# A hybrid decoder step on one core: fewer, longer steps in the mixers' first stage, and small products in four quarters of the array

## The chip, the cores and the metric

The kernel runs on one core of one Trainium2 chip. The metric is the device time of one execution in microseconds (us); the median of the runs is compared. A core has TensorE (PE: matrix products into PSUM, which has eight banks here), VectorE (DVE), ScalarE (ACT), GpSimd (POOL) and SyncE (SP), whose queue issues nearly all DMAs of this kernel. Each engine runs its own instructions in the order in which they were built, and waits on semaphores for the others. TensorE's clock is granted at one of two levels, 1.2 or 2.4 GHz; the profile prints the grant as a share of 2.4 GHz.

## The reference

One layer of a decoder over 2048 prompt tokens and 8 sample tokens, width 1024:

```python
h = rmsnorm(x, norm_mix)
p = h @ w_in                                  # 31 tiles of 128 columns are kept
y_a = gdn_mixer(p_a)     # gated delta rule: conv, decay, chunks of 64, triangular solve
y_b = rwkv_mixer(p_b)    # RWKV-7: token shift, data-dependent decay, state update per token
y_c = hgrn_mixer(p_c)    # forget gate, chunks of 64, gated norm
x = x + concat(y_a, y_b, y_c) @ w_out
h = rmsnorm(x, norm_ffn)
x = x + (silu(h @ w_gate) * (h @ w_up)) @ w_down     # hidden width 2816
y = rmsnorm(x, norm_final)
```

The three mixers carry a 64x64 state per head from chunk to chunk, and the states are outputs too. All is fp32 in and out.

## The kernel before

**Products.** Every large product is done as three fp32r matmuls (hi x hi, hi x lo, lo x hi; lines 377 to 379, in `mm3`), 128x128 weights against up to 512 columns. The tokens are cut into four quarters `q` of 512 (the last has 520, done as two pieces of 260). A quarter has 31 tiles of the input projection (`proj`, tile `psp`), the output projection (`out_proj`, 8 tiles `pso`, which read the mixers' results back from DRAM, `s_mix`, as `mxs`), and the feed-forward part (`ffn`: 22 tiles `pfg` and `pfu`, and `pd`). In matmuls that is 31 x 24 + 8 x 24 + 22 x 48 + 3 x 8 x 22 = 2520 a quarter; counted over the program 7560 of 512 columns and 5040 of 260. All four quarters' projections come first, then for each quarter the output projection and the feed-forward part.

**Mixers.** Each quarter has eight units: three of `gdn` (names with `_g`), three of `rwkv` (`_r`), two of `hgrn` (`_h`); the digits in a built name are the quarter and the unit, so `px_g22` belongs to quarter 2, unit 2. A unit is a Python generator with a first stage (all that needs no state: `first()`), for `gdn` and `rwkv` a stage that inverts 64x64 triangles through DRAM (`inverse`), a second stage that walks the eight chunks in a chain (`px`, `pv`, `pS`, each a small matmul and then a VectorE step), and an output part. Each `yield` ends a step. The eight sample tokens have units of their own (`gs`, `rs`, `hs`), started beside quarter 2's.

**Order.** `Driver.turn` lets each live unit take one step, at most one unit (for the third kind of stage two) in a stage, and then asks the products' generator for as many matmuls as `RATES[q]` says:

```python
        self.due += self.rate
        while self.made < self.due and self.product():
            pass
```

`RATES` (line 1428) is 12.25, 14.25, 15.25 and 19.25 for the four quarters. A quarter's output projection is asked for only when its units are done (`D.left[q]`). This written order is a priority and not yet the order of the engines: the recording layer lays the instructions out on a planned timeline (`schedule_with_timeline_sim=True`), where TensorE takes a later product whenever the earlier small matmuls are not ready. The order that comes out of this is fixed in the program.

**Small matmuls.** They are fp32, and the hardware runs each as two passes, so the trace has two records for one. Their operands have 64 or 32 partitions and sit in a part of the array: partitions 0 to 63 of a 64x64 operand with PSUM partitions 0 to 63 take one quarter of the array, 64 to 127 with 64 to 127 the quarter diagonal to it. `pair` (line 255 on) does head 0 and head 1 of a pair in those two quarters. `hgrn` has five levels (spans 32, 16, 8, 4, 2), each a scaled copy `lv`, eight pairs into one bank `pl`, and one predicated copy on VectorE (line 1217). `rwkv` makes `pa` in the two diagonal quarters and, later, `pk` in the two others. First-stage tiles in PSUM share two banks (tag `A`).

Of the kernel before, what the change touches and what calls it, by code (L numbers as in the profile page):

```python
# [14 lines left out]
ALU = mybir.AluOpType  # L15
# [10 lines left out]
C = 64  # L26
G = 512
GC = G // C
# [63 lines left out]
class Kern:  # L92
# [645 lines left out]
    def half(self, pair, h, other=False):  # L738

        return self.heads(pair[h], other)(h)  # L740
# [39 lines left out]
    def gdn(self, q, u):  # L780

        nc = self.nc
# [5 lines left out]
        def first():  # L788
# [17 lines left out]
            sums, made = {}, None  # L806
# [26 lines left out]
            yield  # L833
# [3 lines left out]
            nc.vector.scalar_tensor_tensor(t, beB, -1.0, L, ALU.mult, ALU.mult)  # L837
            N = ch(self.T(f"N_{nm}"))

            Q = [ch(self.T(f"Q{h}_{nm}")) for h in range(2)]  # L840
            for c0 in range(0, GC, 4):
# [7 lines left out]
                yield  # L849
            inv = self.inverse(N, ("g", u, q), nm)  # L850
            next(inv)
            yield
# [7 lines left out]
            yield  # L860
# [3 lines left out]
            nc.vector.tensor_tensor(ch(dl), k3, ch(dl), ALU.mult)  # L864
            kd = ch(self.T(f"kd_{nm}"))
# [110 lines left out]
    def rwkv(self, q, u, lo):  # L976
# [7 lines left out]
        def first():  # L984
# [6 lines left out]
            nc.tensor.matmul(ps, lhsT=self.w2a2[0:64, us], rhs=wa[0:64], start=True, stop=True)  # L991
            self.rwkv_decay(lw, ps, u)
            nc.vector.tensor_tensor_scan(cu, self.reset, lw, 0.0, ALU.mult, ALU.add)
            yield
# [13 lines left out]
            yield  # L1008
# [3 lines left out]
            a = self.T(f"a_{nm}")  # L1012
            ps = self.ps(f"paa_{nm}")
            nc.tensor.matmul(ps, lhsT=self.w2a2[64:128, us], rhs=wa[64:128], start=True, stop=True)
            self.rwkv_rate(a, ps, u)
            yield
# [21 lines left out]
            def att(l3, swap, outs, name):  # L1038

                for c0 in range(0, GC, 4):  # L1040
                    ps = self.ps(f"p{name}_{nm}").rearrange("p (c w i) -> p c w i", w=2, i=C)
                    for c in range(4):
# [4 lines left out]
                    for w in range(2):  # L1047
                        for to, p in outs(w):
                            to, at, n = to[:, c0:c0 + 4], ps[p, :, w], p.stop - p.start
                            m = lambda x: x[p, None, :].to_broadcast([n, 4, C])  # L1050
                            if w == 0:
                                nc.vector.tensor_tensor(to, at, m(self.nstrict), ALU.mult)
                            else:
                                nc.vector.scalar_tensor_tensor(to, m(self.neg), 0.0, at, ALU.is_ge, ALU.mult)
                    yield

            NR = [ch(self.T(f"{n}_{nm}")) for n in ("N", "Rb")]
            yield from att(a3, 0, lambda w: ((NR[w], slice(0, 128)),), "a")
            N, Rb = NR
            inv = self.inverse(N, ("r", u, q), nm)  # L1060
            next(inv)
            yield

            W = [[ch(self.T(f"W{w}{h}_{nm}")) for h in range(2)] for w in range(2)]
            yield from att(k3, 1, lambda w: [(half(W[w], h, True), slice(64 - 64 * h, 128 - 64 * h))
                                             for h in range(2)], "k")
# [7 lines left out]
            self.tr_tok(self.heads(kt, True), k, f"ptk_{nm}")  # L1074
            yield
# [7 lines left out]
            nc.vector.tensor_tensor(a3, a3, fb, ALU.mult)  # L1083
            yield
# [78 lines left out]
    def hgrn(self, qi, u):  # L1163
# [7 lines left out]
        def first():  # L1171
# [27 lines left out]
            yield  # L1199
            for n, s in enumerate((32, 16, 8, 4, 2)):  # L1200
# [12 lines left out]
                yield  # L1213
                ps = ch(self.ps(f"pl_{nm}"))
# [8 lines left out]
            for h in range(2):  # L1223
                nc.vector.tensor_tensor(half(W, h), ch(q)[H[h]], ch(eb)[H[h]], ALU.mult)
                nc.vector.tensor_copy(half(W, h, True), att[H[h]])
# [202 lines left out]
RATES = (12.25, 14.25, 15.25, 19.25)  # L1428
# [224 lines left out]
```

## Time and profile before

| what | before |
|---|---|
| median of 3 runs | 3200.33 us (3198.95 to 3200.74) |
| profiled execution | 3198.47 us, its span 3196.7 us |
| TensorE busy | 3085.4 us, 97% of the span |
| VectorE busy | 2192.8 us, 69% |
| ScalarE busy | 1189.0 us, 37% |
| mean granted clock | 0.983 |

The span runs from the first to the last instruction; the profiled execution's own time lies 1.8 us over it. Busy time of TensorE is the union of its matmuls, whose ends are modelled: a matmul of 512 columns is shown as some 0.39 us long while the next starts after 0.23. So costs on TensorE are read from one start to the next, not from the durations.

### The profile page before, as it was taken

How to read it: one execution, taken by the hardware profiler on the slowest of the kernel's cores; microseconds unless marked ns; L12 is line 12 of the kernel's file. 1: busy time of each engine (PE TensorE's matmuls, PEld its weight loads, DVE VectorE, ACT ScalarE, POOL GpSimd, SP SyncE). 2: the span in 40 equal slices, each digit the busy share in tenths (PEclk: the TensorE clock that was granted, in tenths of full speed). 3: DMA queues.
4: the chain of work that ended last, by engine and by line, in shares of the span. 5: the costliest groups of instructions: out<-in, count | busy, mean ns of one | idle time of the engine just before them, and what ended most of it. 6: DMA issues, size and time to landing. Idle time of an engine off the chain costs nothing.

```text
span 3196.7 us, 62530 instructions
## 1 busy us (share of the span) xinstructions
PE 3085.4 (97%) x24812; PEld 2469.9 (77%) x24812; DVE 2192.8 (69%) x5369; ACT 1189.0 (37%) x2056; POOL 10.2 (0%) x21
## 2 busy tenths in 40 slices
PE   5989999999999999999999999999999999999998
PEld 3767767777888767677777777777777778999998
DVE  4885666678667788986898887778766654443334
ACT  3543143235325444644365435254532312221002
POOL 0000000000000000000000000000000000000000
PEclk8989999999999999999999999999999999999999
DMA  9958657656655766677775445565645456755552
GB/s 233 333 187 272 186 177 215 187 167 183 198 162 184 229 212 204 221 226 251 227 226 185 162 158 170 168 184 183 205 162 165 149 207 210 249 173 185 185 185 90
DMA packets 393074, 628.06 MB, mean 196 GB/s; under 512 B 176653, under 2 KB 181005, under 8 KB 392781
## 3 DMA queue, kind: packets, MB, share of 16 engines
q1 hardware_dynamic: 391692, 622.99, 61.0%
q8 instruction: 195, 3.19, 0.4%
q10 hardware_dynamic: 1088, 1.07, 0.1%
q14 instruction: 99, 0.80, 0.1%
HBM read 456.79 MB, written 167.19 MB: 195 GB/s over the span
## 4 chain that ended last, share of the span: by engine, by line
PE 79%; DVE 9%; DMA 6%; ACT 3%; SPq 1%; issue 1%; DVEq 0%; ACTq 0%
PE psp L377 7%; PE psp L378 7%; PE psp L379 7%; PE pd L377 5%; PE pd L378 5%; PE pd L379 5%; PE pfu L378 5%; PE pfg L377 4%; PE pfu L377 4%; PE pfu L379 4%; PE pfg L378 4%; PE pfg L379 4%; PE pso L378 1%; PE pso L377 1%; PE pso L379 1%
## 5 line engine op out<-in xcount | busy, mean ns | idle before, releaser
L377 PE MATMUL psp<-xs,w_in 128*128 128x512 f32 (+1 forms) x1240 | 446.3, 360 | 29.2 <-ACT xs L409 17.5
L378 PE MATMUL psp<-xs,w_in 128*128 128x512 f32 (+1 forms) x1240 | 445.9, 360 | 0.3 <-DVE xs L410 0.3
L379 PE MATMUL psp<-xs,w_in 128*128 128x512 f32 (+1 forms) x1240 | 442.9, 357 | 0.8 <-DVE w_in L333 0.8
L377 PEld LDWEIGHTS psp<-xs,w_in 128*128 128x128 f32 x1240 | 235.5, 190 | 72.6 <-ACT xs L409 19.7
L379 PEld LDWEIGHTS psp<-xs,w_in 128*128 128x128 f32 x1240 | 235.6, 190 | 39.5 <-issue 4.4
L378 PEld LDWEIGHTS psp<-xs,w_in 128*128 128x128 f32 x1240 | 235.4, 190 | 39.1 <-issue 2.9
L591 DVE TENSOR_TENSOR x<-pd,x 128x512 f32<-128x512 f32 (+1 forms) x240 | 138.3, 583 | 115.6 <-PE pd L379 113.9
L377 PE MATMUL pfg<-xhs,w_wg 128*128 128x512 f32 x496 | 201.8, 407 | 3.9 <-ACT w_wg L332 2.3
L379 PE MATMUL pfu<-xhs,w_wu 128*128 128x512 f32 x496 | 198.7, 401 | 1.4 <-DVE w_wu L333 1.2
L378 PE MATMUL pfg<-xhs,w_wg 128*128 128x512 f32 x496 | 198.6, 400 | 0.7 <-DVE xhs L549 0.7
L378 PE MATMUL pfu<-xhs,w_wu 128*128 128x512 f32 x496 | 199.2, 402 | 0.0
L377 PE MATMUL pfu<-xhs,w_wu 128*128 128x512 f32 x496 | 198.6, 400 | 0.3 <-ACT w_wu L332 0.3
L379 PE MATMUL pfg<-xhs,w_wg 128*128 128x512 f32 x496 | 198.0, 399 | 0.8 <-DVE w_wg L333 0.8
L377 PE MATMUL pd<-u,w_wd 128*128 128x512 f32 x464 | 188.3, 414 | 6.4 <-ACT u L362 2.3
L378 PE MATMUL pd<-u,w_wd 128*128 128x512 f32 x464 | 187.2, 404 | 0.4 <-DVE u L363 0.2
L379 PE MATMUL pd<-u,w_wd 128*128 128x512 f32 x464 | 185.1, 400 | 0.0
L570 ACT ACTIVATE t<-t 128x512 f32<-128x512 f32 (+1 forms) x110 | 60.0, 546 | 305.3 <-DVE t L569 301.7
L286 ACT ACT_TABLE_LOAD x91 | 116.8, 1283 | 113.6 <-PE oss_g L276 22.1
L362 ACT ACTIVATE u<-t 128x512 fp32r<-128x512 f32 (+1 forms) x110 | 59.9, 545 | 221.1 <-DVE t L573 220.2
L473 DVE TENSOR_TENSOR p<-psp,ri 128x512 f32<-128x512 f32 (+1 forms) x155 | 90.3, 583 | 73.2 <-PE psp L379 71.3
L572 DVE SCALAR_TENSOR_TENSOR t<-pfu,rf 128x512 f32<-128x512 f32 (+1 forms) x110 | 64.2, 583 | 102.9 <-PE pfu L379 100.0
L569 DVE TENSOR_TENSOR t<-pfg,rf 128x512 f32<-128x512 f32 (+1 forms) x110 | 64.2, 584 | 91.3 <-PE pfg L379 83.2
(638 smaller groups left out, 7368.9 us busy)
## 6 DMA issues: line engine op xcount, KB each, us to landing
w_in<-sw_in SPq DMA_DIRECT2D x186, 512.0 KB, 3.9
w_wg<-sw_wg SPq DMA_DIRECT2D x80, 512.0 KB, 3.5
w_wu<-sw_wu SPq DMA_DIRECT2D x80, 512.0 KB, 3.3
w_wd<-sw_wd SPq DMA_DIRECT2D x72, 512.0 KB, 3.3
sw_in<-w_in SPq DMA_DIRECT2D x62, 512.0 KB, 5.1
s_p<-p SPq DMA_DIRECT2D x93, 256.0 KB, 4.3
sw_wg<-w_wg SPq DMA_DIRECT2D x44, 512.0 KB, 2.9
sw_wu<-w_wu SPq DMA_DIRECT2D x44, 512.0 KB, 3.7
```

The lines of the kernel that those rows point to most:

```text
L286: p = self.nc.scalar.preload_act_table_set("natural_log_exp_and_others")
L362: nc.scalar.activation(out[:, 0], src, AF.Copy)
L377: nc.tensor.matmul(ps, lhsT=hi[:, ws], rhs=xs[:, 0, xc], start=start, stop=False)
L378: nc.tensor.matmul(ps, lhsT=hi[:, ws], rhs=xs[:, 1, xc], start=False, stop=False)
L379: nc.tensor.matmul(ps, lhsT=lo[:, ws], rhs=xs[:, 0, xc], start=False, stop=stop)
L473: nc.vector.tensor_tensor(p[:, c0:c0 + cn], ps, rstd[q][:, c0:c0 + cn], ALU.mult)
L569: nc.vector.tensor_tensor(g, psg, r[:, cs], ALU.mult)
L570: nc.scalar.activation(t, g, AF.Tanh, scale=0.5)
L572: nc.vector.scalar_tensor_tensor(p, psu, 0.5, r[:, cs], ALU.mult, ALU.mult)
L591: nc.vector.tensor_tensor(x2[d][:, c0:c0 + cn], ps, x2[d][:, c0:c0 + cn], ALU.add)
```

## The change

It rewrites the first stage of all mixers in 78 steps a quarter instead of 118 (yields are taken out, and what stood between them runs on), and raises `RATES` so that more matmuls are asked for after a turn. In `gdn` the sum of squares of one part is started behind the convolution of the next. In `rwkv` the rate `a` is made beside the decay, and `pa` and `pk` are made in one loop, in turns, into two banks, which fills all four quarters of the array. In `hgrn` a level's scaled copy is made one step ahead, and its pairs go to two banks: even chunks in the diagonal quarters, odd chunks in the other two; so there are two predicated copies of half the size, and the final copies `W` are split in two. No matmul is added or taken away.

```diff
@@ gdn first
+            def total():
+                which, sq = pend
+                sums[which] = self.bsum(f"ss_{nm}", sq), sq
+                return made or self.mm
...
-                yield
+                if pend:
+                    made = total()
                 self.gate(x, x)
                 if which < 2:
                     sq = self.T(f"sq_{nm}")
                     nc.scalar.activation(sq, x, AF.Square)
-                    sums[which] = self.bsum(f"ss_{nm}", sq), sq
-                    made = made or self.mm
-                    yield
+                    pend = which, sq
+                yield
...
@@ rwkv first
+            for c0 in range(0, GC, 4):
+                cs = slice(c0, c0 + 4)
+                pa, pk = (self.ps(f"p{x}_{nm}").rearrange("p (c w i) -> p c w i", w=2, i=C) for x in "ak")
+                for c in range(4):
+                    for ps, l3, swap in ((pa, a3, 0), (pk, k3, 1)):
                         for h in range(2):
-                            p, o = slice(64 * h, 64 * h + 64), 64 * (h ^ swap)
-                            nc.tensor.matmul(ps[o:o + 64, c], lhsT=l3[p, c0 + c], rhs=rk[p, :, c0 + c],
+                            nc.tensor.matmul(ps[H[h ^ swap], c], lhsT=l3[H[h], c0 + c], rhs=rk[H[h], :, c0 + c],
                                              start=True, stop=True)
...
@@ hgrn first
+            x3 = level(32)
+            yield
+            for n, s in enumerate((16, 8, 4, 2, 0)):
+                now, x3 = x3, level(s) if s else None
+                ps = [self.ps(f"pl{i}_{nm}")[:, :G // 2].rearrange("p (c i) -> p c i", i=C) for i in range(2)]
                 for c in range(GC):
-                    self.pair(lambda p: ps[p, c], lambda p: x3[p, c], lambda p: x3[p, c])
-                nc.vector.copy_predicated(att, self.bc(self.msk[:, n]), ps)
+                    for h in range(2):
+                        nc.tensor.matmul(ps[c % 2][H[h ^ c % 2], c // 2], lhsT=now[H[h], c], rhs=now[H[h], c],
+                                         start=True, stop=True)
+                for i in range(2):
+                    nc.vector.copy_predicated(att[:, i::2], self.bc(self.msk[:, n], GC // 2), ps[i])
                 yield
...
-RATES = (12.25, 14.25, 15.25, 19.25)
+RATES = (16.5, 19.0, 18.0, 25.5)
```

What this does to the built order is shown at three places. **First place, TensorE, quarter 2's output projection.** Before, the first tile `pso2_0` stands among small matmuls of quarter 3 (`r30`, `g31`):

```order
L379 MATMUL pso2_0_24683<-mxs2_3_24657,w_o_0_2_24677 128x512
L377 MATMUL pso2_0_24683<-mxs2_4_24661,w_o_0_2_24679 128x512
L260 MATMUL pS_r30_24576<-SA_r30_23454,bt_r30_22875 64x64 x2
L378 MATMUL pso2_0_24683<-mxs2_4_24661,w_o_0_2_24679 128x512
L379 MATMUL pso2_0_24683<-mxs2_4_24661,w_o_0_2_24679 128x512
L377 MATMUL pso2_0_24683<-mxs2_5_24665,w_o_0_2_24679 128x512
L882 MATMUL px_g31_24581<-Z0_g31_24313,kb_g31_23603 64x64
```

Now it stands among those of quarter 2 itself (`h20`, `g22`, `r22`), whose results it reads; after six matmuls of `pso2_1` no product follows for 143 rows:

```order
L378 MATMUL pso2_1_25101<-mxs2_1_25027,w_o_1_2_25095 128x512
L379 MATMUL pso2_1_25101<-mxs2_1_25027,w_o_1_2_25095 128x512
L1229 MATMUL pl0_h20_19261<-lv_h20_19153 64x64 x8
L1229 MATMUL pl1_h20_19262<-lv_h20_19153 64x64 x8
L713 MATMUL pj_r22_19236<-N_r22_18074,uT_r22_18882 32x32 x16
L499 MATMUL pny1_0_25131<-sqhy1__25127,ones_118 128x512
L1381 MATMUL pw_rs0_19854<-lora_s_19839,w2a2_113 128x8
L1229 MATMUL pl0_h20_19326<-lv_h20_19255 64x64 x8
L260 MATMUL pv_r22_19758<-X_r22_19695,N_r22_18074 64x64
```

So at the same product the mixers are three to four of the eight units further back. **Second place, SP's queue, the same projection.** Before, all of `s_mix2` is stored, the last being `y_h21`, before the first load `mxs2_0`, and the loads stand together:

```order
L514 DMA mxs2_0_24645<-s_mix2_156 128x512
L514 DMA mxs2_1_24649<-s_mix2_156 128x512
L514 DMA mxs2_2_24653<-s_mix2_156 128x512
L347 DMA w_wd_5_1_1_24443<-sw_wd_5_1_0_0_18729 128x1024
L514 DMA mxs2_3_24657<-s_mix2_156 128x512
```

Now each load stands right behind the store that it waits for, here at the end:

```order
L744 DMA s_mix3_157<-y_hs0_22466 128x8
L1308 DMA S0_hs1_22528<-st_h 128x8x64
L485 DMA z_g30_24313<-s_p3_150 128x512
L744 DMA s_mix2_156<-y_h21_22501 128x512
L514 DMA mxs2_7_25051<-s_mix2_156 128x512
```

The loads now come one by one, as the mixers' results do. **Third place, TensorE, the products in four quarters.** An `hgrn` level of quarter 0 was eight pairs in a row:

```order
L260 MATMUL pl_h00_5184<-lv_h00_5120 64x64 x15
L260 MATMUL pl_h00_5338<-lv_h00_5226 64x64 x9
L695 MATMUL pj_r02_5083<-inD_206,uT_r02_4964 32x32 x32
L260 MATMUL pl_h00_5338<-lv_h00_5226 64x64 x7
L260 MATMUL pl_h00_5419<-lv_h00_5371 64x64 x16
```

Now the two banks `pl0` (diagonal quarters) and `pl1` (the others) change after every pair here:

```order
L1229 MATMUL pl0_h00_4960<-lv_h00_4901 64x64 x2
L1229 MATMUL pl1_h00_4961<-lv_h00_4901 64x64 x2
L1229 MATMUL pl0_h00_4960<-lv_h00_4901 64x64 x2
L1229 MATMUL pl1_h00_4961<-lv_h00_4901 64x64 x2
L1229 MATMUL pl0_h00_4960<-lv_h00_4901 64x64 x2
```

In quarter 2, as the rows of the first place show, and in most of `pa` and `pk`, the recording layer has put the eight of one bank ahead of the eight of the other: there only two quarters are at work at a time, as before.

## Rows read from the trace of the kernel before

**Rows 1.** The page: busy time by engine; busy tenths in 40 slices.

```profile
span 3196.7 us, 62530 instructions
...
PE 3085.4 (97%) x24812; PEld 2469.9 (77%) x24812; DVE 2192.8 (69%) x5369; ACT 1189.0 (37%) x2056; POOL 10.2 (0%) x21
...
PE   5989999999999999999999999999999999999998
...
DVE  4885666678667788986898887778766654443334
...
PEclk8989999999999999999999999999999999999999
```

**Rows 2.** The page: shares of the chain that ended last, by engine.

```profile
PE 79%; DVE 9%; DMA 6%; ACT 3%; SPq 1%; issue 1%; DVEq 0%; ACTq 0%
```

**Rows 3.** Timeline: start, us, engine, line, tiles; products, and small matmuls between them.

```profile
2150.61 0.40 PE L378 MATMUL pfu<-xhs,w_wu 128*128 128x512 f32 x1
2150.85 0.39 PE L379 MATMUL pfu<-xhs,w_wu 128*128 128x512 f32 x1
2151.17 0.33 PE L894 MATMUL pS_g<-Z_g,kd_g 64*64 64x64 f32 x4
2151.43 0.50 PE L377 MATMUL pfu<-xhs,w_wu 128*128 128x512 f32 x1
...
2156.84 0.40 PE L377 MATMUL pfg<-xhs,w_wg 128*128 128x512 f32 x1
2157.16 0.33 PE L882 MATMUL px_g<-Z_g,kb_g 64*64 64x64 f32 x4
2157.33 0.28 PE L260 MATMUL pS_r<-SA_r,bt_r 64*64 64x64 f32 x4
2157.54 0.50 PE L378 MATMUL pfg<-xhs,w_wg 128*128 128x512 f32 x1
...
3002.05 0.28 PE L379 MATMUL pfu<-xhs,lw_wu 128*128 128x260 f32 x1
3002.17 0.28 PE L377 MATMUL pfu<-xhs,hw_wu 128*128 128x260 f32 x1
```

**Rows 4.** Windows: stretch, its length, busy us (and instructions) by engine, clock, DMA.

```profile
165.96:196.96 31.00, 21.13 (x360) 14.47 (x358) 30.14 (x77) 16.88 (x30) 0.00 (x0) 0.72 0.28 73
196.96:214.00 17.04, 17.04 (x65) 12.78 (x66) 14.47 (x36) 11.39 (x17) 0.00 (x0) 0.82 0.98 358
480.00:2232.00 1752.00, 1707.27 (x14580) 1327.08 (x14579) 1385.15 (x3491) 778.71 (x1361) 3.16 (x6) 0.99 0.62 196
800.00:1200.00 400.00, 385.85 (x4010) 323.83 (x4008) 303.86 (x841) 162.77 (x325) 0.53 (x1) 0.98 0.63 197
1200.00:1600.00 400.00, 388.65 (x2908) 290.59 (x2908) 333.28 (x797) 191.99 (x328) 0.53 (x1) 1.00 0.70 226
2232.00:2260.00 28.00, 26.94 (x175) 20.11 (x174) 21.75 (x56) 6.07 (x10) 0.00 (x0) 1.00 0.69 214
```

**Rows 5.** Timeline of TensorE in the one stretch without products, and behind it.

```profile
165.48 0.40 PE L379 MATMUL psp<-xs,w_in 128*128 128x512 f32 x1
165.72 0.40 PE L276 MATMUL bss_r<-lo_bss_r,blkr 128*128 128x512 f32 x1
165.96 0.60 PE L724 MATMUL ptv_r<-cst,vr 128*128 128x128 f32 x4
...
167.60 1.91 PE L438 MATMUL psb<-raw_x,wba 128*12 128x512 f32 x16
169.44 1.31 PE L1045 MATMUL pa_r<-kr_r,a_r 64*64 64x128 f32 x20
...
172.58 1.09 PE L1045 MATMUL pk_r<-kr_r,kr 64*64 64x128 f32 x16
...
196.96 0.79 PE L377 MATMUL psp<-xs,w_in 128*128 128x512 f32 x1
...
199.54 0.63 PE L379 MATMUL psp<-xs,w_in 128*128 128x512 f32 x1
199.97 0.63 PE L377 MATMUL psp<-xs,w_in 128*128 128x512 f32 x1
```

**Rows 6.** Timeline: a part of an hgrn level; one unquartered product of 512 columns in two passes.

```profile
601.38 0.56 PE L260 MATMUL pl_h<-lv_h 64*64 64x64 f32 x12 [0.33 <-DVE att_h L1217]
...
2153.59 1.12 PE L991 MATMUL pw_r<-wa,w2a 64*128 64x512 f32 x2
2154.64 0.50 PE L377 MATMUL pfg<-xhs,w_wg 128*128 128x512 f32 x1
```

**Rows 7.** Groups by line: line, engine, tiles, passes or instructions; busy us, mean ns; idle before.

```profile
L260 PE MATMUL pl_h<-lv_h 64*64 64x64 f32 x1280 | 50.1, 223 | 0.9 <-DVE att_h L1217 0.9
...
L1045 PE MATMUL pk_r<-kr_r,kr 64*64 64x128 f32 x384 | 26.7, 274 | 1.0 <-DVE Rb_r L1054 1.0
...
L1217 DVE COPY_PREDICATED att_h<-msk,pl_h 128x512 f32<-128x512 uint8 x40 | 29.1, 727 | 4.6 <-PE pl_h L260 4.3
```

More of the change, by code (lines that the diff above doesn't have):

```diff
@@ L848, in first @@
                     nc.vector.tensor_tensor(half(Q, h, True)[:, cs], ps[H[h], :, 1], L3[H[h], cs], ALU.mult)
-                yield
+            yield
             inv = self.inverse(N, ("g", u, q), nm)
             next(inv)
-            yield
             eg = self.T(f"eg_{nm}")
@@ L864, in first @@
             nc.vector.tensor_tensor(ch(dl), k3, ch(dl), ALU.mult)
+            yield
             kd = ch(self.T(f"kd_{nm}"))
@@ L991, in first @@
             nc.tensor.matmul(ps, lhsT=self.w2a2[0:64, us], rhs=wa[0:64], start=True, stop=True)
+            a = self.T(f"a_{nm}")
+            psa = self.ps(f"paa_{nm}")
+            nc.tensor.matmul(psa, lhsT=self.w2a2[64:128, us], rhs=wa[64:128], start=True, stop=True)
             self.rwkv_decay(lw, ps, u)
             nc.vector.tensor_tensor_scan(cu, self.reset, lw, 0.0, ALU.mult, ALU.add)
+            self.rwkv_rate(a, psa, u)
             yield
@@ L1011, in first @@
             nc.scalar.activation(d, d, AF.Exp, scale=-1.0)
[L1012 to L1016, printed above, removed]
             k = self.shifted(q, T_R + 3 * u + 1, 3 + u, f"k{nm}")
@@ L1036, in first @@
             fb = f[:, :, None].to_broadcast([128, GC, C])
[L1038 to L1042, printed above, removed]
+            N, Rb = (ch(self.T(f"{n}_{nm}")) for n in ("N", "Rb"))
+            W = [[ch(self.T(f"W{w}{h}_{nm}")) for h in range(2)] for w in range(2)]
+            for c0 in range(0, GC, 4):
[3 more added lines that the diff above has]
+                    for ps, l3, swap in ((pa, a3, 0), (pk, k3, 1)):
@@ L1043, in att @@
                         for h in range(2):
-                            p, o = slice(64 * h, 64 * h + 64), 64 * (h ^ swap)
-                            nc.tensor.matmul(ps[o:o + 64, c], lhsT=l3[p, c0 + c], rhs=rk[p, :, c0 + c],
+                            nc.tensor.matmul(ps[H[h ^ swap], c], lhsT=l3[H[h], c0 + c], rhs=rk[H[h], :, c0 + c],
                                              start=True, stop=True)
[L1047 to L1059, printed above, removed]
+                def out(to, ps, w, p):
+                    m = lambda x: x[p, None, :].to_broadcast([p.stop - p.start, 4, C])
+                    if w == 0:
+                        nc.vector.tensor_tensor(to[:, cs], ps[p, :, w], m(self.nstrict), ALU.mult)
+                    else:
+                        nc.vector.scalar_tensor_tensor(to[:, cs], m(self.neg), 0.0, ps[p, :, w], ALU.is_ge, ALU.mult)
@@ L1060, in first @@
+                for w, to in enumerate((N, Rb)):
+                    out(to, pa, w, slice(0, 128))
+                for w in range(2):
+                    for h in range(2):
+                        out(half(W[w], h, True), pk, w, H[1 - h])
+                yield
             inv = self.inverse(N, ("r", u, q), nm)
             next(inv)
[L1062 to L1066, printed above, removed]
@@ L1074, in first @@
             self.tr_tok(self.heads(kt, True), k, f"ptk_{nm}")
+            nc.vector.tensor_tensor(a3, a3, fb, ALU.mult)
             yield
@@ L1198, in first, with level @@
             nc.gpsimd.memset(att, 0.0)
-            yield
-            for n, s in enumerate((32, 16, 8, 4, 2)):
+            def level(s):
                 half_ = lambda x: x.rearrange("p (n w s) -> p n w s", w=2, s=s)
@@ L1212, in first @@
                 x3 = ch(x)
-                yield
-                ps = ch(self.ps(f"pl_{nm}"))
-                for c in range(GC):
-                    self.pair(lambda p: ps[p, c], lambda p: x3[p, c], lambda p: x3[p, c])
-                nc.vector.copy_predicated(att, self.bc(self.msk[:, n]), ps)
+                return x3
+            x3 = level(32)
+            yield
+            for n, s in enumerate((16, 8, 4, 2, 0)):
+                now, x3 = x3, level(s) if s else None
+                ps = [self.ps(f"pl{i}_{nm}")[:, :G // 2].rearrange("p (c i) -> p c i", i=C) for i in range(2)]
+                for c in range(GC):
+                    for h in range(2):
+                        nc.tensor.matmul(ps[c % 2][H[h ^ c % 2], c // 2], lhsT=now[H[h], c], rhs=now[H[h], c],
+                                         start=True, stop=True)
+                for i in range(2):
+                    nc.vector.copy_predicated(att[:, i::2], self.bc(self.msk[:, n], GC // 2), ps[i])
                 yield
@@ L1224, in first @@
                 nc.vector.tensor_tensor(half(W, h), ch(q)[H[h]], ch(eb)[H[h]], ALU.mult)
-                nc.vector.tensor_copy(half(W, h, True), att[H[h]])
+                for i in range(2):
+                    nc.vector.tensor_copy(half(W, h, True)[:, i::2], att[H[h ^ i], i::2])
             ends = self.sp.tile([128, GC], F32, tag="he", name=f"he_{nm}")
```

7 lines of the change are left out of this document (1 added, 6 removed).

## The prediction

> **What bounds the kernel now.** I read the page first: TensorE is busy 97% of the span, VectorE 69% [rows 1], and 79% of the chain that ended last runs over TensorE [rows 2]. So time is TensorE's work plus its waits. Then the timeline, from one start to the next: products of 512 columns follow each other every 0.233 us, those of 260 every 0.12 [rows 3]. With 7560 and 5040 of them the products alone are 1761 + 605 = 2366 us. TensorE is idle for 3197 - 3085 = 111 us [rows 1]; the remaining 720 us are the 12212 passes of small matmuls (24812 less 12600), 0.059 us each with all they cause. Last the windows: of the idle time only 45 us lie between 480 and 2232 us, and the clock there is 0.99 [rows 4].
>
> One stretch matters most. From 165.96 to 196.96 us TensorE has no product to run [rows 5]. There it is busy 21 of 31 us at a mean clock of 0.72, and VectorE is busy 30.1 of the 31 [rows 4]: without products the mixers run as fast as VectorE can, 77 instructions in 31 us, 0.403 us each. Behind it the clock is still low (0.82 to 214 us), and products stand 0.43 us apart [rows 4, 5]. Where the kernel reaches quarter 2's output projection (2232 us) nothing of this kind happens: TensorE is busy 26.9 of 28 us [rows 4].
>
> **The change, part by part.** The matmuls are the same, 19006 in either program. What moves is where they stand.
>
> *The stall it brings.* In the new order quarter 2's output projection is reached while the mixers of that quarter still run; its products need `s_mix2`, so TensorE has none. I followed the waits in the built program. When TensorE has passed the sixth matmul of `pso2_1` (the 7284th product), VectorE can at most have done 3588 of its 5425 instructions, because the next one reads a `pl` that TensorE makes later; the first matmul of `pso2_3` (the 7345th product) needs 4173 of them done. Before, the same two points are 4273 and 4305. So 585 VectorE instructions must run, one after another, while TensorE has 61 products and some 1520 passes. Price of VectorE: 0.403 us as in the stretch; these 585 have fewer of the long ones (197 of 512 columns, a third, against 44% there), and by the trace's durations for their shapes they average 0.422 us against 0.442, so 0.385: 225 us. TensorE's own work there, which it would have anyway, is 61 x 0.233 + 1520 x 0.059 = 104 us, of which I take 100. The loss is 125 us, and 8 us more for products at half clock behind it (17 us at 0.43 instead of 0.233, as at 197 us). Ends: 0.361 us an instruction, the lowest busy time of a long window (303.86 / 841), gives 211, a loss of 111; 0.418 (333.28 / 797) gives 245 and, with the 8, a loss of 153 [rows 4]. I take 133, since the stretch is the only row of the same situation. ScalarE isn't the bound there: 16.9 of the 31 us.
>
> *A second, smaller one.* At product 8723 (in `pd2`) the order holds 86 VectorE instructions, some of an `hgrn` level and of a chain, ahead of the next product, and 47 small matmuls, some 12 us: 86 x 0.385 = 33, a loss of 21. Ends 15 and 25.
>
> *Fewer interruptions.* A lone pair between two products costs 0.58 - 0.233 = 0.35 us, one that follows another of the same shape adds 0.12 [rows 3]. So the same work in one interruption less saves 0.23. The order has 638 interruptions of the products, 720 before: 82 x 0.23 = 19 us, gained. Ends: 10 (0.12, the price of a further pair) and 29 (0.35).
>
> *Four quarters.* Today a `pl` pass takes (0.56 - 0.22) / 11 = 0.031 us in two quarters [rows 6, 7], a `pk` pass (1.09 - 0.27) / 15 = 0.054 [rows 5, 7]. A pass of 512 columns in one place takes (2154.64 - 2153.59) / 2 = 0.52 [rows 6]; the sixteen of `psb`, four column places at a time, take (169.44 - 167.60) / 16 = 0.115 [rows 5]. So places do run side by side, even on the same partitions, and four quarters should halve a pass. But the built order has only 433 of 640 `pl` matmuls and 74 of 384 `pa` and `pk` among neighbours from four quarters: 866 x 0.0155 + 148 x 0.027 = 17 us. I take 14, gained; ends 0 and 17. The Trainium skill (TensorE: Matmul & The Clock Gate, Part 3) says that a weight load overlaps running matmuls only when their row groups differ; every third matmul of the new rows has the row group of the first, so by that rule the gain would be 0. The 0.115 of `psb`, all on the same rows, speaks against it.
>
> *Waits elsewhere.* Up to 2232 us there are 45 us of idle time and, at clock 0.99, some 17 us lost to half clock [rows 4]. With products further ahead of the mixers TensorE finds one more often; with VectorE at fewer instructions by then (3557 instead of 4247 at the first `pso2`) it is waited for less. I take 10 us gained; ends 52 gained and 20 lost.
>
> *At nothing.* The halved predicated copies (80 instead of 40; the old ones take 0.727 us each [rows 7]) and the split `W` copies add 56 short instructions to VectorE, some 8 us; outside of the stalls the products cover them, and in the stalls they are among the 585 and 86. Both banks of tag `A` are now taken by a level, so its matmuls wait for both copies of the level before; between them stand products. The sum of squares in `gdn` that starts four VectorE instructions (3 us) later lies under the same cover. Loads of `mxs2` in SP's queue now wait for a store ahead of them, and the mixers' loads queue behind; that is inside the stall, and would lengthen it.
>
> Sum against the profiled execution: 3198.5 + 133 + 21 - 19 - 14 - 10 = 3309.5. The median of the runs lies 2 us above that execution; I say 3310.
>
> **The rivals.** *A longer stall.* The chain of a unit (`px`, `pv`, `pS`, each waiting for VectorE) at half clock, and the loads behind the stores, could keep VectorE from 97%: at 0.5 us an instruction the 585 take 293, and the time is 3310 + 68 = 3378. For it: TensorE would run 100 us of work at half speed. Against: in the stretch at 166 us, with more TensorE work per us, VectorE still had 97%.
>
> *The quarters don't overlap.* 3310 + 14 = 3324.
>
> *On the other side: products ahead pay.* If in the first 2080 us TensorE, always with a product at hand, loses all its waits (52 gained instead of 10), interruptions save 29, and the stall runs at 0.361 with no half clock behind it (111 instead of 133), the sum is 3310 - 42 - 10 - 22 - 6 - 3 = 3227 with the second stall at its low end and the quarters at theirs: still slower. To reach 3192 the stall would have to cost no more than 76, that is 585 instructions at 0.30 us, less than any window shows for VectorE. It decides if VectorE's instructions, none waiting for another, follow each other faster than in any long stretch of this trace. Time then 3190.
>
> *It doesn't do what it says* in part: the steps are fewer, but most `pa` and `pk` don't use four quarters; that is in the sum.
>
> **How the numbers follow.** Forecast (a stall of 111 to 153, other terms between their ends) 0.80, around 3310, from 3255 to 3345; longer stall 0.10, 3378; quarters without overlap 0.05, 3324; the other side 0.05, 3190 to 3227. The range 3245 to 3350 leaves out most of the longer stall and of the other side, and the far corners of the sum. A measurement of this kernel tells about 0.2% (6.4 us) from no change. Faster 0.03, same 0.02, slower 0.95, all from the other side's share.
>
> **What would show it.** In the changed kernel's slices TensorE falls to 4 to 6 tenths for some 225 us from about 2085 us on, with the clock between 0.5 and 0.8 and VectorE at 9; a window there shows some 585 VectorE instructions at 0.36 to 0.42 us. A shorter dip follows near 2750. Up to 2085 the idle time is 50 to 90 us, as before. `pl` passes of quarters 0 and 1 start some 0.016 apart, those of quarter 2 0.03. I am wrong if TensorE keeps 9 tenths through that place, or if VectorE is well below 90% in it, so that something else (SP's queue, chains at half clock) holds the mixers.

## The result and the profile after

The changed kernel is slower: 3385.93 us, median of 4 runs (3382.03 to 3388.45), against 3199.64 us for four runs of the kernel before. The ratio is 1.0587, interval 1.0566 to 1.0607. The forecast was 3310 us, range 3245 to 3350: right in sign and place, too small by 76 us, and outside its range.

The page of the changed kernel, as [rows 1] and [rows 2] show the one before: busy time by engine, busy tenths in 40 slices of 84.5 us, chain by engine.

```profile
span 3380.2 us, 62720 instructions
...
PE 3131.1 (93%) x24812; PEld 2496.6 (74%) x24812; DVE 2199.6 (65%) x5425; ACT 1209.4 (36%) x2073; POOL 10.5 (0%) x21
...
PE   6989999999999999999999999556999998999998
...
DVE  5883663768748768688837748977794666443334
...
PEclk8989999999999999999999999565999998999999
...
PE 71%; DVE 13%; DMA 8%; ACT 4%; issue 2%; SPq 1%; DVEq 0%; ACTq 0%
```

Everything is as in [rows 1] but for one hole: in slices 26 to 28 TensorE is busy 5 to 6 tenths, at a granted clock of 0.5 to 0.6. VectorE, which the forecast had at 9 tenths there, is at 9, 7 and 7. A shallow second dip follows in slice 34. On the chain VectorE, DMA and ScalarE take the share that TensorE lost.

The windows say more. Columns as in [rows 4]: stretch, its length, busy us and instructions of TensorE, its weight loads, VectorE, ScalarE and GpSimd, then clock, DMA share, GB/s. First the changed kernel, up to the last product before the hole (the 7284th), in the hole, behind it, and in the second dip.

```profile
0.00:2111.90 2111.90, 2012.10 (x15704) 1557.18 (x15704) 1459.53 (x3586) 834.00 (x1426) 3.89 (x12) 0.98 0.66 209
2112.00:2385.00 273.00, 161.56 (x1547) 109.98 (x1546) 219.63 (x591) 129.31 (x219) 0.52 (x1) 0.58 0.22 59
2385.00:2420.00 35.00, 35.00 (x245) 25.79 (x243) 25.15 (x76) 15.73 (x30) 0.00 (x0) 1.00 0.66 222
2804.00:2865.00 61.00, 45.83 (x451) 35.69 (x450) 43.90 (x125) 15.90 (x26) 0.52 (x1) 0.75 0.34 117
```

The kernel before, up to the same product:

```profile
0.00:2235.50 2235.50, 2142.46 (x17596) 1647.96 (x17597) 1708.21 (x4270) 966.10 (x1668) 4.17 (x13) 0.98 0.65 203
```

From these rows the 183.5 us of span (3380.2 less 3196.7) divide into three, if small passes are again priced at 0.059 us each (the last row ends with the last product, 14 us before the end in both):

| stretch | before | after | small passes before, after | net, by this count | forecast |
|---|---|---|---|---|---|
| up to the 7284th product | 2235.5 us | 2111.9 us | 10312, 8420 | 124 ahead, 112 of it passes left for later: 12 gained | 43 gained |
| from there to the first of `pso2_3` | 21.8 us | 272.8 us | 86, 1484 | 251 more, 82 of it the passes left over: 169 lost | 133 lost |
| the rest | 925.2 us | 981.0 us | 1808, 2302 | 56 more, 29 of it passes: 27 lost | 21 lost |

So what is lost behind the first stall came near its forecast; the first stall costs 36 us more than forecast, and of the gains 31 us did not arrive.

The edges of the hole, on TensorE (start, duration, line, tiles): products 0.23 us apart, then small matmuls; and, 235 us later, products inside the hole.

```profile
2111.66 0.40 PE L378 MATMUL pso<-mxs,w_o 128*128 128x512 f32 x1
2111.89 0.40 PE L379 MATMUL pso<-mxs,w_o 128*128 128x512 f32 x1
2112.22 0.97 PE L1229 MATMUL pl_h<-lv_h 64*64 64x64 f32 x32
...
2348.09 0.63 PE L379 MATMUL pso<-mxs,w_o 128*128 128x512 f32 x1
2348.52 0.63 PE L378 MATMUL pso<-mxs,w_o 128*128 128x512 f32 x1
```

Inside, products stand 0.43 us apart, as behind the stretch of [rows 5]. Behind the hole nothing is slow: the window from 2385 us on has a clock of 1.00.

**What VectorE does in the hole.** It runs 591 instructions (585 were forecast) and is busy 219.6 us (225 were forecast, idle moments included). But it is busy only 80% of the 273 us, where the stretch of [rows 4] had 97%. An instruction comes every 0.462 us instead of 0.385. That is 48 us more, and nearly all of it is idle VectorE: 53 us, where 7 were forecast. (The loss is only 36 us over the forecast: the 8 us for half clock behind the stall were not there, and TensorE's own work came to 104 us by the count above, where 100 were taken.) What VectorE waited for in the hole (engine, line and tile that waits; who ended the wait; us in total, times, longest), the costliest rows:

```profile
DVE cols_hs L1161 <- ACT cols_hs L1160: 8.5, 2, 5.2
DVE kq_g L778 <- ACT th L777: 6.8, 3, 2.5
DVE cols_rs L1151 <- ACT yt_rs L300: 4.7, 2, 2.8
DVE ga_mo_hs L1296 <- PE mo_hs L276: 3.7, 1, 3.7
DVE mxs L363 <- ACT mxs L362: 3.5, 2, 2.5
```

Four of the five are waits for ScalarE. Of the 46 us that VectorE's waits of this table make in all, ScalarE ended 35 and TensorE 10. One place, VectorE's timeline first, the idle time before an instruction in brackets:

```profile
2249.47 0.18 DVE L670 TENSOR_TENSOR inU_g<-inU_g,inT_g 64x14 f32<-64x14 f32 x1
2251.59 0.23 DVE L1151 SCALAR_TENSOR_TENSOR cols_rs<-cols_rs,par_t,yt_rs 128x8 f32<-128x8 f32 x1 [1.94 <-ACT yt_rs L300]
...
2255.65 0.17 DVE L1161 TENSOR_SCALAR cols_hs<-cols_hs 128x8 f32<-128x8 f32 x1 [3.31 <-ACT cols_hs L1160]
...
2258.43 0.75 DVE L939 SCALAR_TENSOR_TENSOR kr<-pkr,par_t,kr 128x512 f32<-128x512 f32 x1 [1.84 <-ACT kr L938]
```

and ScalarE's:

```profile
2249.01 0.63 ACT L1020 ACTIVATE d_r<-d_r 128x512 f32<-128x512 f32 x1
2249.75 1.28 ACT L286 ACT_TABLE_LOAD   x1
2251.05 0.27 ACT L297 ACTIVATE yt_rs<-yv_rs,par_t 128x8 f32<-128x8 f32 x1
...
2254.11 1.28 ACT L1160 ACT_TABLE_LOAD   x1 [2.56 <-DMA s_mix<-cols_rs]
2255.41 0.21 ACT L1160 ACTIVATE cols_hs<-smp 128x8 f32<-128x8 f32 x1
...
2256.28 1.28 ACT L1165 ACT_TABLE_LOAD   x1
```

ScalarE loads a function table (1.28 us) whenever it goes between tanh and logarithm, 34 times in the hole, 44 us. Here it does so for the sample units (`rs`, `hs`), whose tiles have eight columns: a chain of short steps. The first step of `hs` also waits 2.56 us until a result of `rs` is stored: the sample units' columns share two buffers (`cols`, line 1284). VectorE stands still for 7 of 9 us. The Trainium skill (ScalarE: Activation LUTs, "What ACT_TABLE_LOAD costs") counts 2.66 us for a change of table, 1.28 for the load and 1.38 for draining the engine. The load agrees; the draining is not to be seen here: the load starts 0.11 us behind the activation before it and the next one 0.02 us behind the load.

This gave three questions: which part of the change makes the stall, what keeps VectorE at 80% in it, and where the gains went.

### The profile page after: what moved, and what is told of

The parts are those of the page before. It is cut to its first block, busy times and chain, and to the rows that moved or that the text cites. A ratio compares the mean times of both kernels' runs of the same rounds, so it can differ in the third digit from the quotient of the medians.

```text
span 3380.2 us, 62720 instructions
## 1 busy us (share of the span) xinstructions
PE 3131.1 (93%) x24812; PEld 2496.6 (74%) x24812; DVE 2199.6 (65%) x5425; ACT 1209.4 (36%) x2073; POOL 10.5 (0%) x21
## 4 chain that ended last, share of the span: by engine, by line
PE 71%; DVE 13%; DMA 8%; ACT 4%; issue 2%; SPq 1%; DVEq 0%; ACTq 0%
PE psp L377 7%; PE psp L378 6%; PE psp L379 6%; PE pfu L377 4%; PE pfu L378 4%; PE pfu L379 4%; PE pfg L378 4%; PE pd L377 4%; PE pfg L377 4%; PE pfg L379 4%; PE pd L378 4%; PE pd L379 4%; PE pso L377 1%; PE pso L378 1%; PE pso L379 1%
## 5 line engine op out<-in xcount | busy, mean ns | idle before, releaser
L377 PE MATMUL pd<-u,w_wd 128*128 128x512 f32 x488 | 196.2, 411 | 9.5 <-ACT u L362 3.1
L378 PE MATMUL pd<-u,w_wd 128*128 128x512 f32 x488 | 197.3, 404 | 2.1 <-DVE u L363 2.1
L379 PE MATMUL pd<-u,w_wd 128*128 128x512 f32 x488 | 195.6, 401 | 0.0
```

Source lines behind the costliest of these rows:

```text
L377: nc.tensor.matmul(ps, lhsT=hi[:, ws], rhs=xs[:, 0, xc], start=start, stop=False)
L378: nc.tensor.matmul(ps, lhsT=hi[:, ws], rhs=xs[:, 1, xc], start=False, stop=False)
L379: nc.tensor.matmul(ps, lhsT=lo[:, ws], rhs=xs[:, 0, xc], start=False, stop=stop)
```

## Experiments: which part of the change makes the stall

**Only the new RATES, on the kernel before.**

```diff
-RATES = (12.25, 14.25, 15.25, 19.25)
+RATES = (16.5, 19.0, 18.0, 25.5)
```

> The kernel before with the new RATES (16.5, 19, 18, 25.5) alone; its steps and small products are untouched. Theory (products run ahead of the mixers because more of them are asked for after a turn): TensorE again finds no product at quarter 2's output projection, and a second time about product 9056. By the built order VectorE must there do 81 and 42 us more than TensorE has work; in the changed kernel 107 us by the same count became 179, so these 123 become 123 to 205 us; 120 mode switches of the array fewer give back 22. Time 3300 to 3383. Rival (the stall comes from the steps made fewer and longer, or from the four quarters): no stall, 3175 to 3200.

Measured: 3397.73 us, ratio 1.0633 (1.0614 to 1.0652). Slices, and windows up to the 7284th product and in the two holes:

```profile
PE   5989999999999999999999999568999996699998
...
DVE  5875667665568787877667778877424578443334
```

```profile
0.00:2111.20 2111.20, 2026.47 (x16009) 1569.26 (x16010) 1508.54 (x3691) 826.09 (x1436) 4.17 (x13) 0.98 0.67 210
2111.20:2322.60 211.40, 127.93 (x1260) 87.46 (x1258) 174.75 (x460) 111.23 (x190) 0.00 (x0) 0.60 0.26 68
2794.90:2900.20 105.30, 70.15 (x912) 52.70 (x911) 91.48 (x266) 41.85 (x70) 1.05 (x2) 0.60 0.17 46
```

The stall is there without one changed step or product, at the same product, and a second one at quarter 3's output projection. The time lies 15 us over the upper end of the expectation.

**The same, two quarters at a time.** First the rates of quarters 0 and 1, then those of 2 and 3.

```diff
-RATES = (12.25, 14.25, 15.25, 19.25)
+RATES = (16.5, 19.0, 15.25, 19.25)     # first run
+RATES = (12.25, 14.25, 18.0, 25.5)     # second run
```

> The kernel before with the new RATES for quarters 0 and 1 alone (16.5, 19, 15.25, 19.25). If the rate of the two quarters ahead is what puts the products past quarter 2's mixers, the first stall is back: by the built order 381 VectorE instructions from the 7284th product on and 66 us of VectorE too much; at the 0.46 us an instruction that the stalls of the changed kernel and of the run with all four RATES took, a loss of 105 to 126 us. A smaller one near product 9065 (17 us by the order, twice that by the stalls so far: 32), 111 mode switches fewer, 21 back: 3313 to 3334. If the price were the forecast's 0.385: 3270 to 3285. If the rates of quarters 2 and 3 make the stall: 3175 to 3200.

> The kernel before with the new RATES for quarters 2 and 3 alone (12.25, 14.25, 18, 25.5). No stall at quarter 2's output projection; one near product 9033, at quarter 3's, where VectorE must by the order do 23 us too much, with the factor of about 1.9 of the stalls so far 43 us: 3235 to 3245. If it is hidden: 3195 to 3200.

Measured: 3341.21 us (ratio 1.0451, 1.0420 to 1.0481) and 3255.94 us (1.0184, 1.0154 to 1.0213); the kernel before beside them 3197.75. In the first, the hole at quarter 2's output projection is back, and a shorter one at quarter 3's:

```profile
PE   6989999999999999998999999667999998699998
...
2130.60:2315.80 185.20, 111.42 (x1040) 73.72 (x1039) 147.20 (x386) 91.95 (x159) 0.00 (x0) 0.60 0.27 70
...
2809.60:2846.50 36.90, 19.18 (x186) 13.58 (x184) 32.44 (x94) 17.30 (x26) 0.52 (x1) 0.58 0.37 117
```

In the second TensorE keeps 9 tenths up to 2700 us and dips only at quarter 3's output projection:

```profile
2699.90:2766.80 66.90, 43.70 (x642) 33.16 (x641) 59.23 (x157) 32.27 (x52) 0.53 (x1) 0.70 0.24 77
```

Both came out dearer than expected, by 7 and 11 us, and the losses add up: 143 and 58 are 201 us; with all four rates it was 201 (3397.73 less 3196.95). Counted as in the table of the changed kernel, the runs divide so:

| stretch | RATES of all four | of quarters 0, 1 | of quarters 2, 3 |
|---|---|---|---|
| up to the 7284th product | 31 gained | 25 gained | 0 |
| from there to the first of `pso2_3` | 129 lost | 110 lost | 2 gained |
| the rest | 101 lost | 54 lost | 61 lost |

So the first stall is made by the rates of the quarters ahead of it; what is lost behind it comes from both pairs, about half of it from each.

**The new steps with the old RATES.**

```diff
-RATES = (16.5, 19.0, 18.0, 25.5)
+RATES = (12.25, 14.25, 15.25, 19.25)
```

> The changed kernel with the old RATES (12.25, 14.25, 15.25, 19.25). If RATES alone were wrong for the new steps, this is free of the stall: about 3165 to 3185. If the longer steps by themselves put mixers and products in another order (by the built order one stretch is left, near product 6896, in quarter 1's feed-forward part, where VectorE must do 215 us more than TensorE has work): 3380 to 3520.

Measured: 3562.8 us, ratio 1.1138 (1.1117 to 1.1159). Slices, and the window of the one long hole:

```profile
PE   6989999999999999989999765556699999999998
```

```profile
2011.00:2587.50 576.50, 338.69 (x4014) 232.44 (x4012) 460.51 (x1326) 258.96 (x441) 2.11 (x4) 0.55 0.15 35
```

Between two products of quarter 1's feed-forward part TensorE's order now holds 4014 passes of small matmuls without a product, for 577 us, 43 us over the expected time at the end. It is the other side of the same balance: a turn asks for `RATES[q]` matmuls, so fewer turns at the old rate ask for fewer products, and the mixers are written ahead of products that come after them in one block, which goes at VectorE's pace. So the rates had to rise with the steps cut, and raised they bring the stall.

**Only the products in four quarters.** The kernel before, its RATES and its number of steps, with `pa` and `pk` in one loop and `pl` in two banks:

```diff
+            for c0 in range(0, GC, 4):
...
+                pa, pk = (self.ps(f"p{x}_{nm}").rearrange("p (c w i) -> p c w i", w=2, i=C) for x in "ak")
...
             next(inv)
             yield
...
+            yield
+            yield
...
-                ps = ch(self.ps(f"pl_{nm}"))
+                ps = [self.ps(f"pl{i}_{nm}")[:, :G // 2].rearrange("p (c i) -> p c i", i=C) for i in range(2)]
...
```

> The kernel before with its own RATES and as many steps, but pa and pk in one loop into two banks and pl in two banks, as in the change. The order has no stretch where VectorE is behind by more than before. If four quarters run side by side: 992 of the 1280 pl passes at 0.0155 instead of 0.031 us (15 us), 252 pa and pk passes at 0.037 instead of 0.055 (4 to 5 us), 29 mode switches fewer (5 us): 3175, faster than before by 0.8%. If quarters on the same rows do not overlap: 3194 to 3200. If the doubled predicated copies or the second bank of tag A cost on the path: 3205 or more.

Measured: 3178.96 us, median of 9 runs (3173.47 to 3189.74), ratio 0.9950 (0.9938 to 0.9963): faster than both kernels.

```profile
span 3171.7 us, 62591 instructions
...
PE   5999999999999999999999999999999999999998
```

No hole; 25 us less of span in the profiled execution, 18 us in the medians, where 22 were expected. Four quarters pay, by themselves.

**The other way round: `pl` back in two quarters**, the rest of the change kept.

```diff
-                ps = [self.ps(f"pl{i}_{nm}")[:, :G // 2].rearrange("p (c i) -> p c i", i=C) for i in range(2)]
+                ps = ch(self.ps(f"pl_{nm}"))
                 for c in range(GC):
-                    for h in range(2):
-                        nc.tensor.matmul(ps[c % 2][H[h ^ c % 2], c // 2], lhsT=now[H[h], c], rhs=now[H[h], c],
-                                         start=True, stop=True)
-                for i in range(2):
-                    nc.vector.copy_predicated(att[:, i::2], self.bc(self.msk[:, n], GC // 2), ps[i])
+                    self.pair(lambda p: ps[p, c], lambda p: now[p, c], lambda p: now[p, c])
+                nc.vector.copy_predicated(att, self.bc(self.msk[:, n]), ps)
...
```

> The changed kernel with hgrn's pl back in one bank and two quarters (steps, RATES, pa and pk as changed). If the quarters' gain is real, it loses some 13 us of it (866 passes by 0.0155). If the second bank also put the mixers further back at quarter 2's output projection (by the built order 83 + 11 us of VectorE too much there instead of 107 + 16), it wins 30 to 50 us at that place: together 3350 to 3370, below the changed kernel. If the stall has nothing to do with the quarters: 3395 to 3400.

Measured: 3381.58 us, ratio 1.0578 (1.0561 to 1.0594), 4 us under the changed kernel and between the two expectations. Windows up to the 7284th product and in the hole:

```profile
0.00:2148.10 2148.10, 2037.46 (x15937) 1580.42 (x15938) 1491.56 (x3644) 849.22 (x1448) 3.89 (x12) 0.97 0.65 206
2148.00:2385.60 237.60, 134.53 (x1316) 92.90 (x1314) 183.46 (x486) 116.71 (x195) 0.53 (x1) 0.59 0.23 60
```

The hole is 35 us shorter in these windows, as expected (30 us from the 7284th product to the first of `pso2_3`). But the product ahead of it is reached 36 us later, with only 233 more passes done (14 us): 22 us of the quarters' gain and of waits are gone (idle time 110.6 against 99.8 us). The two effects cancel within 4 us, so the second bank has a small part in the length of the stall and none in its being there.

## Experiments: what keeps VectorE at 80% in it

**No function tables.** Every tanh becomes a copy, the explicit loads go.

```diff
-        with self.tables(made or self.mm) if load else ExitStack():
+        with ExitStack():
...
-        self.nc.scalar.activation(th, x, AF.Tanh, scale=0.5)
+        self.nc.scalar.activation(th, x, AF.Copy, scale=0.0)
...
```

> The changed kernel with every tanh replaced by a scaled copy (scale 0, no bias) and the explicit loads of the logarithm's table left out, so that ScalarE changes its function table hardly ever; the numbers computed are others, the instructions and the written order the same. In the stall of the changed kernel ScalarE loads a table 34 times at 1.28 us, 44 us of 273, and VectorE is idle 53 us, mostly for ScalarE. The built order holds 567 VectorE instructions here instead of 585. Theory (ScalarE and its table loads keep VectorE from its own pace): 0.39 to 0.42 us each, stall 220 to 240, VectorE over 88% busy in it, time 3330 to 3355. Rival (chains through a TensorE at half clock keep it): 0.467 each, stall 265, VectorE at 80%, time 3370 to 3385.

Measured: 3335.34 us, ratio 1.0433 (1.0400 to 1.0467).

```profile
2090.20:2335.80 245.60, 151.42 (x1508) 103.91 (x1507) 214.63 (x569) 85.10 (x183) 0.52 (x1) 0.60 0.26 68
```

The hole took 246 us, between the two expectations (220 to 240, 265), VectorE 87% busy: 31 us idle instead of 53. So table loads make some 20 us of the 53. The time of the theory, 3330 to 3355, was met for another reason too: the 7284th product is reached 22 us earlier, so tables cost there as well.

**The loads of `mxs` off ScalarE's queue.**

```diff
-            self.split(t[:, :, :n], raw)
+            nc.gpsimd.tensor_copy(t[:, 0, :n], raw)
+            nc.vector.tensor_tensor(t[:, 1, :n], raw, t[:, 0, :n], ALU.subtract)
```

> The changed kernel with the first half of the split of mxs in the output projections on GpSimd instead of ScalarE, so that ScalarE's queue no longer waits there for loads that follow a store (11.7 us in the stall). The built order holds 601 VectorE instructions in the stall instead of 585. If the blocked ScalarE queue costs VectorE that time: stall 265 to 270, time 3365 to 3378. If it is hidden: 0.467 each, stall 281, time 3390 to 3395. If the slower GpSimd copy is late itself: over 3395.

Measured: 3406.63 us, ratio 1.0656 (1.0622 to 1.0691).

```profile
2138.30:2417.60 279.30, 163.79 (x1598) 111.89 (x1597) 229.93 (x613) 132.93 (x222) 5.14 (x7) 0.60 0.23 63
```

0.456 us an instruction, VectorE at 82%, 49 us idle: as before. ScalarE's wait for the loads costs VectorE next to nothing; this suspicion falls. (The loads still stand behind the stores in SP's queue; no run changed that.) The 21 us more in time go with the 7284th product, which comes 26 us later.

**The sample units beside quarter 3.**

```diff
-            if q == 2:
+            if q == 3:
                 D.side(samples.pop(0), 3)
```

> The changed kernel with the units of the eight sample tokens started beside quarter 3's units instead of quarter 2's. In the stall at quarter 2's output projection the built order then holds 283 VectorE instructions instead of 585, with a second stretch of 241 to 376 from product 8974 on. If the single chains of the sample units (norms, table loads, loads from DRAM) make an instruction cost 0.467 us: the first stall runs at 0.385 to 0.40, 109 to 113 us, with VectorE over 90%, and the second, which has them now, at 0.45 to 0.48. If half clock makes it: 0.467 in both, the first 132 us with VectorE at 80%. Time, by the sum: a first loss of 109 to 132 less 57 us of TensorE's work, a second of 100 to 135, with 21 us fewer for switches: 3330 to 3400.

Measured: 3422.88 us, ratio 1.0707 (1.0668 to 1.0747), over the range.

```profile
2111.60:2240.00 128.40, 78.04 (x664) 53.14 (x663) 110.30 (x287) 64.02 (x99) 0.52 (x1) 0.65 0.30 86
```

The first hole is 128 us, 0.447 an instruction, near the 132 of the other expectation; VectorE is at 86%, between the two. What the sample units brought moved to quarter 3 and cost more there: the stretch from product 8975 to 9163 took 237 us, with VectorE 63% busy.

**Both out together.** Sample units beside quarter 3, and no tables.

> The changed kernel with the sample units beside quarter 3 and without table loads (tanh replaced by a scaled copy, the numbers are others). The order holds 265 VectorE instructions in the first stall. If table loads and sample units each take their own share of VectorE's idle time (13 to 14 per cent of the stall was left with either of them out, 20 with both in): 0.385 to 0.40 us each, 102 to 106 us, VectorE over 93% busy. If what is left with either out is something else, such as chains through TensorE at half clock with few units alive: 0.44 each, 115 to 118 us, VectorE at 86 to 88%.

Measured: 3370.25 us, ratio 1.0541 (1.0511 to 1.0572).

```profile
2088.70:2205.30 116.60, 73.39 (x659) 52.03 (x658) 105.04 (x271) 45.66 (x84) 0.53 (x1) 0.68 0.32 96
```

116.6 us for 271 instructions, 0.430 each, VectorE 90% busy. The size is that of the second expectation, the busy share lies between. With both out, VectorE's gaps of over 1.5 us, 30 us of the 53 in the changed kernel, are gone; what is left, 11.6 us, is 145 gaps of under 0.3 us (5.7 us) and eight longer ones.

All holes side by side:

| kernel | stretch, us | VectorE instructions | us each | VectorE busy |
|---|---|---|---|---|
| changed | 273.0 | 591 | 0.462 | 80% |
| changed, first 116.6 us alone | 116.6 | 287 | 0.406 | 89% |
| RATES alone, quarter 2 | 211.4 | 460 | 0.460 | 83% |
| RATES alone, quarter 3 | 105.3 | 266 | 0.396 | 87% |
| new steps, old RATES | 576.5 | 1326 | 0.435 | 80% |
| new steps, old RATES, last 144.5 us alone | 144.5 | 347 | 0.416 | 78% |
| pl in two quarters | 237.6 | 486 | 0.489 | 77% |
| no tables | 245.6 | 569 | 0.432 | 87% |
| mxs off ScalarE | 279.3 | 613 | 0.456 | 82% |
| samples later | 128.4 | 287 | 0.447 | 86% |
| RATES of quarters 0, 1 | 185.2 | 386 | 0.480 | 79% |
| both out | 116.6 | 271 | 0.430 | 90% |

The hole at quarter 3 with RATES alone has neither sample units nor stored results of theirs, and 7 table loads; at the same clock of 0.60 it runs at 87%. But holes of different length can't be compared by their shares, because the share changes along a hole. The changed kernel's hole in two parts, the first as long as the whole hole with both out; then the last part of the hole of the new steps at the old RATES:

```profile
2112.00:2228.60 116.60, 69.79 (x673) 48.95 (x671) 103.41 (x287) 49.40 (x82) 0.52 (x1) 0.63 0.22 69
2228.60:2385.00 156.40, 91.77 (x874) 61.03 (x875) 116.22 (x305) 79.91 (x137) 0.00 (x0) 0.54 0.21 51
...
2443.00:2587.50 144.50, 97.20 (x1310) 70.74 (x1310) 113.42 (x347) 52.52 (x87) 1.05 (x2) 0.54 0.09 23
```

In its first 116.6 us the changed kernel's VectorE is at 89%, with sample units (53 of the 287 instructions) and 13 table loads in it, hardly less than the 90% with both out; 40 of the 53 us idle lie in the 156 us behind that. So the step from 80% to 90% doesn't price the two. What the runs show is this. Without table loads the same work has 31 us of idle time, so the loads make some 20 of the 53. In the changed kernel 24 us of the 53 stand right before the 120 instructions of the sample units, table loads in part among them, and without these units the hole ends where its emptier part began. And neither is needed: the last row has no instruction of a sample unit on VectorE and 10 table loads, and VectorE is at 78%. There the longest waits end with TensorE's `pv` and `pS`, the chain of the second stage. How much of that is TensorE at half clock was not taken apart: no run kept the clock up in a hole.

## Why the prediction was wrong

**The stall: right in place and cause, its price too low.** Product, instruction count (585, measured 591), clock (0.58), the half-clock spacing of 0.43 us and the shorter second dip came as said. The step that failed is "I take 133, since the stretch is the only row of the same situation". It carried 97% busy over from 31 us at the start to a hole of 273. That stretch has no sample units, but it has steps of the second stage's chain (`px`, `pv`, `pS`), and its 4 table loads stand as close as the 34 of the hole; yet VectorE is idle only 0.9 us there. So neither chains nor loads alone make the difference, and 31 us are too short to tell the mean: the hole's own pieces of 31 us run from 57% to 97%, its first 94%.

```profile
2112.00:2143.00 31.00, 16.59 (x222) 11.41 (x220) 29.28 (x83) 13.84 (x23) 0.00 (x0) 0.63 0.29 103
...
2236.00:2267.00 31.00, 14.17 (x208) 9.18 (x208) 17.81 (x54) 18.98 (x34) 0.00 (x0) 0.50 0.23 53
```

VectorE's busy time was right to 1% (97% of 225 is 218 us; measured 219.6); its idle time was forecast at 7 us and measured at 53. The sign "VectorE well below 90%" that the text named against itself is what happened. The rival "a longer stall" had the price nearly right (0.5, measured 0.462) and the time (3378), with the wrong reasons in part. Of the chains: TensorE, at the end of its chains and elsewhere, ended 10 of the 46 us of waits (what of it half clock made is open); the loads behind the stores cost 4 us at most through ScalarE's queue, and through SP's queue they were not tried. The most, 35 us, are waits for ScalarE, with table loads and the sample units' short steps in them. Neither stood in the text; ScalarE was dismissed by its busy share (16.9 of 31 us), and it is busy only 47% of the hole in which it ended these waits. The 8 us for half clock behind the stall were not there: the clock is 1.00 from 2385 us on.

**The cause of the stall.** The text put it down to the new order as a whole. The runs divide it: the raised RATES alone bring 201 us, the new steps alone another, longer stall; the quarters alone none.

**The second stall** was about right: 21 forecast, 27 measured for all behind the first, which is not the dip alone and lies just over the upper end of 25.

**Fewer interruptions** (19 gained) could not be told apart in the changed kernel. With RATES alone there are 119 fewer up to the 7284th product, at 0.23 us 27 us. That part was by the same count 31 us ahead (124.3 less 1587 passes by 0.059), and 8 of these are idle time (84.7 us instead of 93.0). That leaves 0.19 us each, within the ends and a little under the price.

**Four quarters** (14 gained): right in kind, too small in size. Rows of the changed kernel, `pl` on TensorE with neighbours from four quarters, then `pa` and `pk` in turns:

```profile
666.15 0.69 PE L1229 MATMUL pl_h<-lv_h 64*64 64x64 f32 x32
...
1038.71 0.33 PE L1054 MATMUL pk_r<-kr_r,kr 64*64 64x128 f32 x2
1038.80 0.28 PE L1054 MATMUL pa_r<-kr_r,a_r 64*64 64x128 f32 x2
1038.87 0.28 PE L1054 MATMUL pk_r<-kr_r,kr 64*64 64x128 f32 x2
...
1039.24 0.28 PE L1054 MATMUL pa_r<-kr_r,a_r 64*64 64x128 f32 x2
```

The 32 passes of `pl` take 0.69 us with the last one's 0.22, 0.0154 from start to start against 0.031 in [rows 6]: half, as forecast. From 1038.80 to 1039.24 `pa` and `pk` start sixteen passes, two a row, 0.0275 each: half of 0.054 too; over whole runs of 32, whose ends are not in turns, it is 0.035 to 0.043. Over all passes at full clock that follow one of their kind within 0.3 us, the mean fell from 0.031 to 0.0195 (`pl`) and from 0.054 to 0.045: 1280 by 0.011 and 768 by 0.009 are 21 us. With quarters alone the means are 0.018 and 0.043, by the same count 24 us, and the run gained 18. So the gain of 0 that the prediction drew from the Trainium skill's rule on weight loads (TensorE: Matmul & The Clock Gate, Part 3) is not what was measured here.

**Waits elsewhere** (10 gained) was wrong. Up to the 7284th product TensorE is idle 99.8 us, 93.0 before, although it gets there 124 us sooner. With RATES alone it is 84.7, with quarters alone 95.3, with `pl` back in two quarters 110.6: so neither the products ahead nor the second bank make it wait, and the longer steps are what is left. The run of the new steps with the old RATES agrees: at the 6896th product, ahead of its hole, it has 100.2 us, the changed kernel 99.0, the kernel before 93.0, RATES alone 82.2. (Differences of some 5 us say nothing: with the sample units later it is 104.3 up to the 7284th product.) With the 10 forecast, that is 17 of the 31 us of gains that did not arrive; the rest no run took apart.

**The chances.** The forecast's own case had 0.80 and the longer stall 0.10. With a single stretch of 31 us to rest on, that was too sure, and the upper end should have reached the rival's 3378.

## What to carry to other kernels

Where an order leaves TensorE without products, count the instructions that the engine behind must run, but don't carry the idle share of a short stretch over to a long hole: VectorE was idle 3% of a stretch of 31 us, 6% of the first 31 us of the hole, 20% of all its 273 us and 26% of its later part. A change that cuts steps and raises the pace of the work beside them moves a balance; each half alone lost 201 and 366 us, and the third, independent part (four quarters) was worth taking by itself: 3179 us, 0.5% under the kernel before.

## What was not expected of the hardware

A change of ScalarE's table takes 1.28 us, with 0.13 us around it, and 34 of them in 273 us cost VectorE some 20 us of idle time, while ScalarE itself was busy under half of them. The losses from raising the two pairs of RATES add (143 and 58 us singly, 201 together). Small fp32 passes of 64 columns in all four quarters start 15 ns apart, half of the time in two quarters; those of 128 columns do so only where they stand in turns, 27.5 against 54.
